# Two scalings by a column, the softmax division and the normalisation of the mLSTM heads, issued on ScalarE in a one-core hybrid attention block

## The chip, the cores and the metric

The kernel runs on one core of one Trainium2 chip. The metric is the device time of one execution in microseconds: the median over several runs. One execution was also taken with the hardware profiler. It has its own time and a span (first to last instruction), and the times of single instructions below come from it. PE is TensorE (matmuls), PEld its weight loads, DVE is VectorE, ACT is ScalarE, POOL is GpSimd, SP is SyncE, which only issues transfers here.

## What is computed

One layer of a decoder over 16 meta tokens and 512 tokens of width 1024. The normalised input goes through one wide projection. From its columns two branches are fed, and both end in one output projection. The parts that matter here:

```python
# branch 1: attention with forget gates, 8 heads of 128
p = jax.nn.softmax(jnp.where(causal, scores + decay, -jnp.inf), axis=-1)
out = jnp.einsum('bhqk,bkhd->bqhd', p, v)
ya = (oa * jax.nn.silu(fz)) @ w_a

# branch 2: mLSTM, 4 heads of 512 values
h = num / jnp.maximum(jnp.abs(den), jnp.exp(-m_t))[..., None]
hb = jax.nn.sigmoid(mo) * hb
hb = rms_norm(hb, g_head)                 # per head, over its 512 values
yb = (hb * jax.nn.silu(mz)) @ w_b

merged = jax.nn.sigmoid(ga) * ya + jax.nn.sigmoid(gb) * yb
return x + rms_norm(merged @ w_o, g_post)
```

The change concerns two steps: the division of the softmax by its row sums, and the multiplication of each mLSTM head with the reciprocal root of its mean square.

## The kernel before

Tokens stand on the 128 partitions in four chunks (c = 0 to 3), or channels do where a product is formed transposed. Every fp32 factor is split into a high part, rounded to the fp32 format that PE multiplies fast, and a low part. A product is three matmuls (`mm3`, L150 to L152): high by high, high by low, low by high. The high part is a copy on ACT (L142 or L250), the low part a subtraction on DVE (L144 or L252).

The program runs in this order: the norm of the input (to about 30 us), the four mLSTM heads h = 0 to 3 (to about 516 us), four pairs p = 0 to 3 of attention heads (FoX, to about 842 us), and the projections `w_a` and `w_o`. The instructions are written in the order of the functions, but a tile scheduler sorts them for each engine by what it expects to be ready. So an edit of one line can change the order on every engine. Each engine then works through its queue strictly in order, and waits with everything behind when an operand isn't there.

**mLSTM.** For one head, `value_part` is called with chunks (3, 2), then `mz_part(h, 0)` follows, then `value_part` with (1, 0), then `mz_part(h, 1)`. For each chunk `value_part` multiplies on PE (L790 to L793), divides by the denominator on DVE (L796 to L803, result `ht`), squares and sums on ACT (L807, result `mss`), scales the sum on DVE (L808), raises it to the power -0.5 on POOL (L810, result `mrs`), and multiplies `ht` by that column (L811). `turn_part` transposes the `ht` tiles on PE after the head's last chunk.

**Narrow projections.** `mz_part`, `fq_part`, `fz_part` and `gate_part` (names pz, pfq, pfz, pga, pgb) use `st_unit`, a Strassen form: seven products of half-size blocks instead of eight, with weight parts a, b, c, d. Between the products, ACT takes snapshots of half-finished banks (L314, L318, L322). PE may write on into a bank only when its snapshot is taken. At the end DVE combines the snapshots with the banks (L325, L326, L328).

**FoX.** For each head `prob_part` forms the logits (PE), adds the decay and finds the row minimum of their negation on DVE (L972, result `lt` and `mn`), takes the exponential with its row sum on ACT (L977, `rsum`), inverts the sum on DVE (L978), and writes the probabilities `pn`: the meta columns on POOL (L980), the others on DVE (L982, 128, 256, 384 or 512 columns for c = 0 to 3). `lt` has two buffers, so L972 of chunk c + 2 waits until L980 and L982 of chunk c have read theirs. `ptr_part` transposes `pn` on PE and copies it out on ACT (L1007, L1009; low parts on DVE, L1008, L1010). `fout_part` multiplies with the values (pfo, L1022 to L1024). A projection is placed beside each softmax to keep PE supplied: beside the last head (p = 3, m = 1) stands the gate `ga_part(1)`, behind it `ga_part(2)`. The sigmoids of a gate (L932) need another table on ACT than the exponential, hence an ACT_TABLE_LOAD.

Of the kernel before, what the change touches and what calls it, by code (L numbers as in the profile page):

```python
# [11 lines left out]
AF = mybir.ActivationFunctionType  # L12
ALU = mybir.AluOpType

P = 128
# [3 lines left out]
NM = 16  # L19
# [34 lines left out]
def tile_hybrid_block(ctx: ExitStack, tc: tile.TileContext, x, meta, norm_pre, norm_post, w_in, b_fox_f,  # L54
                      conv_w, conv_b, b_i, b_f, g_head, w_a, w_b, w_o, out):
    nc = tc.nc
    V, S, G, T = nc.vector, nc.scalar, nc.gpsimd, nc.tensor
# [11 lines left out]
    def psum1(name):  # L69
        return pa.tile([P, 512], F32, tag="pa", name=name)  # L70

    def banks(name, n):

        return [psum1(f"{name}_{i}") for i in range(n)]

    def line(pool, name, n=1, parts=P, **kw):

        return pool.tile([parts, -(-n // 16) * 16], F32, name=name, **kw)[:, 0:n]
# [19 lines left out]
    def sb(shape, dt, tag, name, pool=None, **kw):  # L98

        n = 1  # L100
        for d in shape[1:]:
            n *= d
        size = BYTES.get(tag, 4096)
        t = (pool or wk).tile([shape[0], size // (2 if dt == BF16 else 4)], dt, tag=tag, name=name, **kw)[:, 0:n]
        if len(shape) == 3:
            t = t.rearrange("p (a b) -> p a b", a=shape[1])
        elif len(shape) == 4:
            t = t.rearrange("p (a b c) -> p a b c", a=shape[1], b=shape[2])
        return t
# [39 lines left out]
    def mm3(ps, ah, al, bh, bl, start, stop, **kw):  # L149
        T.matmul(ps, ah, bh, start=start, stop=False, **kw)  # L150
        T.matmul(ps, ah, bl, start=False, stop=False, **kw)  # L151
        T.matmul(ps, al, bh, start=False, stop=stop, **kw)  # L152
# [628 lines left out]
    def value_part(h, wpk, v, so, hts, chunks):  # L781
        wh, wl = wpk
        vh, vl, vm = v
        for c in chunks:
            pn = (psum1(f"pna{h}{c}"), psum1(f"pnb{h}{c}"))
            for u in (1, 0):
                o, n = u * 256, 256 + 2 * u
                for j in range(c + 1):
                    s0 = OFF[j] + (c - j) * P
                    T.matmul(pn[u][:, 0:n], wh[:, s0:s0 + P], vh[:, j, o:o + n], start=(j == 0), stop=False)  # L790
                    T.matmul(pn[u][:, 0:256], wh[:, s0:s0 + P], vl[:, j, o:o + 256], start=False, stop=False)
                    T.matmul(pn[u][:, 0:n], wl[:, s0:s0 + P], vh[:, j, o:o + n], start=False, stop=False)
                T.matmul(pn[u][:, 0:n], wh[0:MP, OFFM + c * P:OFFM + (c + 1) * P], vm[0:MP, o:o + n],  # L793
                         start=False, stop=True)
            r = line(wk, f"r{h}{c}", 1, tag="r", bufs=4)
            V.tensor_scalar(r, pn[1][:, 256:257], -1.0, col[:, NB + NCH + c, 8 + h:9 + h], ALU.mult, ALU.max)  # L796
            V.tensor_tensor(r, pn[1][:, 256:257], r, ALU.max)
            V.reciprocal(r, r)
            if c % 2:
                ht2 = sb([P, 2, MV], F32, ("qk0h", "qk0l")[c // 2], f"ht{h}{c}")  # L800
            ht = ht2[:, c % 2, :]
            for u in range(2):
                V.scalar_tensor_tensor(ht[:, u * 256:u * 256 + 256], pn[u][:, 0:256], r,  # L803
                                       so[:, c, u * 256:u * 256 + 256], ALU.mult, ALU.mult)
            junk = sb([P, MV], BF16, "y", f"mjunk{h}{c}", bufs=2)
            ss = line(wk, f"mss{h}{c}", 1, tag="ss", bufs=8)
            S.activation(junk, ht, AF.Square, accum_out=ss)  # L807
            V.tensor_scalar(ss, ss, 1.0 / MV, EPS, ALU.mult, ALU.add)  # L808
            rs = line(wk, f"mrs{h}{c}", 1, tag="rs", bufs=7)
            G.tensor_tensor(rs, ss, mhalf, ALU.pow)  # L810
            V.tensor_scalar(ht, ht, rs, None, ALU.mult)  # L811
            hts[c] = ht

    def turn_part(h, hts, gz):
# [35 lines left out]
    for h in range(MH):  # L850
# [24 lines left out]
        else:  # L875
            wpk = score_part(h, q, k, w)
            so = mo_part(h)
        hts, gz = [None] * NCH, []
        value_part(h, wpk, v, so, hts, (3, 2))
        gz.append(mz_part(h, 0))  # L880
        value_part(h, wpk, v, so, hts, (1, 0))
        gz.append(mz_part(h, 1))
        pend = (h, hts, gz)
# [61 lines left out]
    def prob_part(p, m, q, k):  # L945

        h = 2 * p + m
        qh, ql = q
        kh, kl = k
        ab = sb([P, NA], F32, "ab", f"ab{h}", gp)  # L950
        nc.sync.dma_start(ab, d_na[h:h + 1, :].to_broadcast([P, NA]))
        pn = sb([P, NPACK], F32, "w", f"pn{h}")
        sums = []
        for c in range(NCH):
            kn = NM + (c + 1) * P
            o = OFFA[c] + kn - P
            G.tensor_tensor(ab[:, o:o + P], ab[:, o:o + P], mask_q, ALU.add)
            for s0, s1 in [(0, kn)] if kn <= 512 else [(0, HL), (HL, kn)]:

                if c != 1:  # L960
                    bank = psum1(f"pl{h}{c}{s0}")
                ps = (bank[:, 144:512] if c == 1 else bank)[:, 0:s1 - s0]
                mm3(ps, qh[:, m, c * P:(c + 1) * P], ql[:, m, c * P:(c + 1) * P],
                    kh[:, m, s0:s1], kl[:, m, s0:s1], True, True)
                sums.append((c, s0, s1, ps))
        for c in range(NCH):
            kn = NM + (c + 1) * P
            lt = sb([P, L], F32, "y", f"lt{h}{c}", bufs=2)
            mn = line(wk, f"mn{h}{c}", 2, tag="mn", bufs=4)
            parts = [(s0, s1, ps) for c_, s0, s1, ps in sums if c_ == c]  # L970
            for i, (s0, s1, ps) in enumerate(parts):
                V.tensor_tensor_reduce(out=lt[:, s0:s1], in0=ps, in1=ab[:, OFFA[c] + s0:OFFA[c] + s1],  # L972
                                       op0=ALU.add, op1=ALU.min, scale=1.0,
                                       scalar=3e38 if i == 0 else mn[:, 0:1], accum_out=mn[:, i:i + 1])
            li = len(parts) - 1
            rsum = line(wk, f"rsum{h}{c}", 1, tag="r", bufs=4)
            S.activation(lt[:, 0:kn], lt[:, 0:kn], AF.Exp, bias=mn[:, li:li + 1], scale=-1.0, accum_out=rsum)  # L977
            V.reciprocal(rsum, rsum)  # L978
            o = OFFP[c]
            G.tensor_scalar(pn[:, o:o + P].rearrange("p (g t) -> p g t", g=4),  # L980
                            lt[:, 0:32].unsqueeze(1).to_broadcast([P, 4, 32]), rsum, None, ALU.mult)
            V.tensor_scalar(pn[:, o + P:o + P + kn - NM], lt[:, NM:kn], rsum, None, ALU.mult)  # L982
        return pn

    def ptr_part(p, m, pn):
# [61 lines left out]
    for p in range(FH // 2):  # L1047
        if p:
            q = fq_part(p)
            if p % 2 == 0:  # L1050
                fout_part(*tail)
            k = fk_part(p)
        pn0 = prob_part(p, 0, q, k)
        if p % 2 == 0:
            v = fv_part(p)
        else:
            fz_part(p)
        pt0 = ptr_part(p, 0, pn0)
        pn1 = prob_part(p, 1, q, k)
        if p % 2 == 0:  # L1060
            fz_part(p)
        elif p == 1:
            gb_part(2)
        else:
            ga_part(1)
        fout_part(p, 0, pt0, v)
        pt1 = ptr_part(p, 1, pn1)
        tail = (p, 1, pt1, v)
        if p % 2 == 0:
            gb_part(p + 1)  # L1070
            fout_part(*tail)
# [57 lines left out]
    pn = banks("pout", NCH)  # L1129
# [7 lines left out]
    for u in (2, 3):  # L1137
        w = wchunk(wo, 0, KC, u * 256, 256, f"wo{u}")
        for b in range(NCH):
# [5 lines left out]
            if u == 3:  # L1145
                rs = line(wk, f"ors{b}", 1, tag="rs", bufs=7)
# [34 lines left out]
```

## Time and profile before

| what | value |
|---|---|
| median of 3 runs | 935.91 us (935.9 to 936.01) |
| profiled execution, its own time | 938.23 us |
| its span | 936.4 us |
| mean granted clock of PE | 0.995 |

In a group's row stands: line, engine, operation, output <- inputs, partitions x elements and type, count, then after the bar the busy us, the mean ns of one, the idle us of the engine just before, and what ended that. In a timeline's row stands: start in us, duration in us, engine, line, operation. A row of the waits names the waiting instruction, what released it, and the us in total, the number and the longest. Durations of neighbours on one engine overlap by some 0.1 us because they are pipelined. The mean clock of 0.995 comes from two stretches of 3.41 us at half clock, which begin at 104.41 and 691.50 us.

### The profile page before, as it was taken

To read this page: it belongs to the slowest core of one execution; us is meant where nothing else is said; L and a number is where in the kernel's file an instruction comes from. 1 tells how busy PE (TensorE), PEld (TensorE's weight loads), DVE (VectorE), ACT (ScalarE), POOL (GpSimd) and SP (SyncE) were. 2 spreads that over 40 slices of the span, in tenths; PEclk is the share of its full clock that TensorE was granted. 3 is DMA by queue.
4 is the path that set the end of the run, shared out by engine and by line. 5 is a ranking of instruction groups with operands and counts; after the bars stand their busy time and mean duration, and the time that the engine had idled before them with its cause. 6 is when DMAs were issued, how large, how long until landed. Compare 5 with 4: busy or idle time off the path is not lost.

```text
span 936.4 us, 15730 instructions
## 1 busy us (share of the span) xinstructions
PE 915.1 (98%) x6304; PEld 847.2 (90%) x6304; DVE 670.4 (72%) x1108; ACT 474.5 (51%) x810; POOL 141.6 (15%) x186
## 2 busy tenths in 40 slices
PE   8999899999999999999999999999989999999997
PEld 6998799889998899988999979899988999998887
DVE  6889688448886378873688767587894688995534
ACT  5645556536565255662455425455753464863231
POOL 3053000122101211012020002111421121300000
PEclk9999999999999999999999999999999999999999
DMA  7323133303333123233133335124352124358402
GB/s 230 93 63 118 46 127 90 111 23 91 109 95 101 51 85 91 95 97 90 33 104 112 96 109 162 49 77 152 101 166 76 56 87 136 98 193 302 135 23 91
DMA packets 73539, 97.47 MB, mean 104 GB/s; under 512 B 5237, under 2 KB 56533, under 8 KB 73466
## 3 DMA queue, kind: packets, MB, share of 16 engines
q1 hardware_dynamic: 71400, 92.76, 32.3%
q0 software_dynamic: 576, 2.10, 0.6%
q10 hardware_dynamic: 1490, 1.61, 0.5%
q8 instruction: 49, 0.80, 0.3%
q14 instruction: 24, 0.20, 0.1%
HBM read 90.62 MB, written 5.83 MB: 103 GB/s over the span
## 4 chain that ended last, share of the span: by engine, by line
PE 81%; DVE 9%; ACT 5%; issue 2%; DMA 2%; POOL 1%; DVEq 0%; POOLq 0%; ACTq 0%; SPq 0%
PE pyb L151 3%; PE pyb L150 3%; PE pyb L152 3%; PE pz L150 3%; PE pz L151 3%; PE pz L152 3%; PE pqk L150 3%; PE pqk L152 3%; PE pqk L151 3%; PE pv L150 3%; PE pv L152 3%; PE pv L151 3%; PE po L152 2%; PE po L150 2%; PE po L151 2%
## 5 line engine op out<-in xcount | busy, mean ns | idle before, releaser
L980 POOL TENSOR_SCALAR pn<-lt,rsum 128x128 f32<-128x128 f32 x32 | 29.5, 923 | 136.7 <-DVE rsum L978 99.6
L151 PE MATMUL pyb<-bl,wb_h 128*128 128x512 f32 x128 | 49.8, 389 | 0.0
L152 PE MATMUL pyb<-bh,wb_l 128*128 128x512 f32 x128 | 49.8, 389 | 0.0
L150 PE MATMUL pyb<-bh,wb_h 128*128 128x512 f32 x128 | 49.8, 389 | 0.0
L151 PE MATMUL pv<-wv_l,hh 128*128 128x512 f32 (+1 forms) x128 | 46.6, 364 | 1.5 <-DVE wv_l L144 1.5
L152 PE MATMUL pv<-wv_h,hl 128*128 128x512 f32 (+1 forms) x128 | 46.4, 363 | 0.0
L150 PE MATMUL pv<-wv_h,hh 128*128 128x512 f32 (+1 forms) x128 | 46.4, 362 | 0.0
L695 DVE SCALAR_TENSOR_TENSOR y<-z,gc,y 128x512 f32<-128x512 f32 (+1 forms) x48 | 36.2, 759 | 2.2 <-ACT y L688 1.4
L150 PE MATMUL pfk<-hh,wfk_h 128*128 128x264 f32 x128 | 36.4, 285 | 0.0
L150 PE MATMUL pqk<-hh,wq_h 128*128 128x258 f32 x128 | 36.4, 284 | 0.0
L150 PE MATMUL pqk<-hh,wk_h 128*128 128x264 f32 x128 | 36.3, 284 | 0.0
L151 PE MATMUL pfk<-hl,wfk_h 128*128 128x264 f32 x128 | 36.3, 283 | 0.0
L152 PE MATMUL pqk<-hh,wk_l 128*128 128x264 f32 x128 | 36.3, 283 | 0.0
L152 PE MATMUL pfk<-hh,wfk_l 128*128 128x264 f32 x128 | 36.3, 283 | 0.0
L151 PE MATMUL pqk<-hl,wk_h 128*128 128x264 f32 x128 | 36.2, 283 | 0.0
L152 PE MATMUL pqk<-hh,wq_l 128*128 128x258 f32 x128 | 36.0, 282 | 0.0
L151 PE MATMUL pqk<-hl,wq_h 128*128 128x258 f32 x128 | 36.0, 282 | 0.0
L151 PEld LDWEIGHTS pv<-wv_l,hh 128*128 128x128 f32 x128 | 24.1, 189 | 5.6 <-DVE wv_l L144 1.7
L152 PEld LDWEIGHTS pyb<-bh,wb_l 128*128 128x128 f32 x128 | 24.0, 188 | 5.0
L150 PEld LDWEIGHTS pyb<-bh,wb_h 128*128 128x128 f32 x128 | 24.0, 188 | 4.9
L151 PEld LDWEIGHTS pyb<-bl,wb_h 128*128 128x128 f32 x128 | 24.0, 188 | 4.9
L845 DVE TENSOR_TENSOR yb<-pyb,yb 128x512 f32<-128x512 f32 x24 | 16.5, 687 | 16.6 <-PE pyb L152 16.6
(1810 smaller groups left out, 3651.5 us busy)
## 6 DMA issues: line engine op xcount, KB each, us to landing
wv_r<-in_w_in_dram SPq DMA_DIRECT2D x16, 512.0 KB, 4.8
wo_r<-in_w_in_dram SPq DMA_DIRECT2D x16, 512.0 KB, 3.8
wz_r<-in_w_in_dram SPq DMA_DIRECT2D x16, 512.0 KB, 4.0
wb_r<-in_w_b_dram SPq DMA_DIRECT2D x16, 512.0 KB, 3.4
ab<-d_na SPq DMA_DIRECT2D x8, 672.0 KB, 4.0
wq_r<-in_w_in_dram SPq DMA_DIRECT2D x8, 512.0 KB, 3.9
wk_r<-in_w_in_dram SPq DMA_DIRECT2D x8, 512.0 KB, 4.7
wfq_r<-in_w_in_dram SPq DMA_DIRECT2D x8, 512.0 KB, 3.7
```

What stands on the lines that cost most here:

```text
L150: T.matmul(ps, ah, bh, start=start, stop=False, **kw)
L151: T.matmul(ps, ah, bl, start=False, stop=False, **kw)
L152: T.matmul(ps, al, bh, start=False, stop=stop, **kw)
L695: V.scalar_tensor_tensor(y[:, t0:L], z[:, m, t0 + j:L + j], gc[:, j * 16 + mi:j * 16 + mi + 1], y[:, t0:L], ALU.mult, ALU.add)
L845: V.tensor_tensor(dst, ps[i], dst, ALU.add)
L980: G.tensor_scalar(pn[:, o:o + P].rearrange("p (g t) -> p g t", g=4), lt[:, 0:32].unsqueeze(1).to_broadcast([P, 4, 32]), rsum, None, ALU.mult)
```

## The change

Two instructions of DVE become activations with the identity function on ACT; the scale is the same column as before. The operands, the tiles and the buffers stay.

```diff
@@ value_part
             G.tensor_tensor(rs, ss, mhalf, ALU.pow)
-            V.tensor_scalar(ht, ht, rs, None, ALU.mult)
+            S.activation(ht, ht, AF.Identity, scale=rs)
             hts[c] = ht
@@ prob_part
             G.tensor_scalar(pn[:, o:o + P].rearrange("p (g t) -> p g t", g=4),
                             lt[:, 0:32].unsqueeze(1).to_broadcast([P, 4, 32]), rsum, None, ALU.mult)
-            V.tensor_scalar(pn[:, o + P:o + P + kn - NM], lt[:, NM:kn], rsum, None, ALU.mult)
+            S.activation(pn[:, o + P:o + P + kn - NM], lt[:, NM:kn], AF.Identity, scale=rsum)
         return pn
```

This moves 16 instructions of L811 (4 heads, 4 chunks) and 32 of L982 (8 heads, 4 chunks). DVE has 48 rows fewer and ACT 48 more, 764 for 716. The count of table loads stays at 23. The scheduler also reorders what stands around them.

On ACT in mLSTM head 1, at the first half of `value_part` and the first snapshot of `mz_part` (ht13 and ht12 are the pair of chunks 3 and 2, gz10 the snapshot of the first `mz_part`), the order is now:

```order
 L758 ACTIVATE so1_2240<-po1_1_2242 128x2x256
 L807 ACTIVATE mjunk13_2506,mss13_2507<-ht13_2503 128x512
+L811 ACTIVATE ht13_2503<-ht13_2503,mrs13_2510 128x512
 L807 ACTIVATE mjunk12_2541,mss12_2542<-ht13_2503 128x512
+L811 ACTIVATE ht13_2503<-ht13_2503,mrs12_2545 128x512
 L314 ACTIVATE gz10_2548<-pz10_1_2550 128x512
 L250 ACTIVATE wz11c_h_2738<-wz111_r0_2728 128x1024
```

The two scalings stand ahead of the snapshot L314; before, it followed L807 directly.

On ACT behind the last softmax, between the gates ga1 and ga2 (sga1 is the sigmoid tile of ga1, wga2b_h and wga2c_h are high parts of the weights of ga2):

```order
 L1035 ACTIVATE gh1_9056<-yb_75 128x1024
 L322 ACTIVATE sga1_8767<-pga1_1_8769 128x256
-L250 ACTIVATE wga2b_h_8945<-wga20_r0_8935 128x1024
-L250 ACTIVATE wga2c_h_8949<-wga21_r0_8937 128x1024
 L932 ACT_TABLE_LOAD
 L932 ACTIVATE sga1_8767<-pga1_0_8768 128x512
@@ -664,21 +710,23 @@
 L1007 ACTIVATE pth7_8902<-pt73_8918 128x4x128
 L1009 ACTIVATE ptm7_8904<-pmt7_8905 128x512
+L250 ACTIVATE wga2b_h_8945<-wga20_r0_8935 128x1024
+L250 ACTIVATE wga2c_h_8949<-wga21_r0_8937 128x1024
```

Both splits move from a place ahead of the table load to one behind the sigmoids and the copies of the transposed probabilities.

On PE at ga1 (pfo6 is the attention output of head 6, pga1_1 the bank whose snapshot is taken on ACT):

```order
 L152 MATMUL pga1_0_8768<-hh_71,wga1c_l_8786 128x256
+L1022 MATMUL pfo6_8887<-pth6_8678,fvh2_7734 128x512
+L1023 MATMUL pfo6_8887<-ptl6_8679,fvh2_7734 128x512
+L1024 MATMUL pfo6_8887<-pth6_8678,fvl2_7735 128x512
+L1022 MATMUL pfo6_8887<-pth6_8678,fvh2_7734 128x384
+L1023 MATMUL pfo6_8887<-ptl6_8679,fvh2_7734 128x384
 L150 MATMUL pga1_1_8769<-t4h_1105,wga1c_h_8784 128x256
```

Five matmuls of the attention output come forward, ahead of the product that waits for the snapshot; at gb2 in pair 1 five of pfo2 do the same.

## The prediction

> **What bounds the kernel now.** I read the profile page first, then the waits of PE, then the groups by line and shape, and last the timelines of the places where the two moved operations stand.
>
> ```profile
> span 936.4 us, 15730 instructions
> ...
> PE 915.1 (98%) x6304; PEld 847.2 (90%) x6304; DVE 670.4 (72%) x1108; ACT 474.5 (51%) x810; POOL 141.6 (15%) x186
> ```
>
> PE is busy 98% of the span, so 936.4 - 915.1 = 21.3 us is all that it leaves open, start and end of the program included. DVE is at 72% and ACT at 51%: neither is the bound on average. The change can act only through the moments in which PE waits, and it can close or open such moments. The waits of PE, with total us, number and longest:
>
> ```profile
> PE pfq L150 <- ACT wfq2d_h L250: 1.9, 1, 1.9
> ...
> PE pfq L150 <- ACT fqs L314: 1.2, 3, 0.5
> ...
> PE pgb L150 <- DVE mn L972: 0.6, 1, 0.6
> PE pga L150 <- DVE mn L972: 0.5, 1, 0.5
> ```
>
> The waits are small and single. Several of them end with an ACT instruction: a weight split (L250) or a snapshot of a half-finished product (L314). PE cannot go on until ACT has taken the snapshot. So what counts on ACT is not its 51%, but what stands in its queue ahead of a snapshot or a split.
>
> **The price of the two operations.** Groups by line and shape; behind the bar are busy us, mean ns of one, and the idle time before:
>
> ```profile
> L811 DVE TENSOR_SCALAR ht<-ht,mrs 128x512 f32<-128x512 f32 x16 | 7.8, 487 | 8.7 <-POOL mrs L810 8.7
> ...
> L982 DVE TENSOR_SCALAR pn<-lt,rsum 128x512 f32<-128x512 f32 x8 | 4.0, 501 | 0.2
> ...
> L982 DVE TENSOR_SCALAR pn<-lt,rsum 128x128 f32<-128x128 f32 x8 | 2.3, 288 | 0.3
> ...
> L807 ACT ACTIVATE mjunk<-ht 128x512 bf16<-128x512 f32 x16 | 10.0, 625 | 12.5 <-DVE ht L803 12.5
> ...
> L687 ACT ACTIVATE z<-pqk 128x258 f32<-128x258 f32 x16 | 6.1, 381 | 12.8 <-PE pqk L152 12.7
> ...
> L688 ACT ACTIVATE y<-pqk,gc 128x258 f32<-128x258 f32 x16 | 8.7, 561 | 0.6 <-DVE bl L826 0.5
> ...
> L977 ACT ACTIVATE lt<-lt,mn 128x528 f32<-128x528 f32 x8 | 5.9, 734 | 8.4 <-DVE mn L972 8.4
> ...
> L977 ACT ACTIVATE lt<-lt,mn 128x144 f32<-128x144 f32 x8 | 3.3, 417 | 3.5 <-DVE mn L972 3.5
> ```
>
> DVE loses 16 instructions of 0.487 us at L811, 7.8 us. At L982 it loses 8 each of four widths, from 0.288 us (128 wide) to 0.501 us (512 wide): by the mean of the ends, 32 x 0.39 = 13 us. On ACT the same passes are longer. No activation of before has exactly the new form (512 wide, SBUF to SBUF, scale from a column), so I bound it. L807 is 512 wide with no column operand: 0.625 us. L688 has two column operands (scale and bias) and L687, of the same shape, none: (561 - 381) / 2 = 90 ns for one. So L811 should take 0.625 + 0.09 = 0.71 us, between 0.63 (the column costs nothing) and 0.81 (it costs as much as both). L977 already takes one column operand, and its 528 and 144 columns are 16 more than L982 has. The step per column is (734 - 417) / 384 = 0.83 ns, so L982 takes 0.72 us at 512 and 0.40 at 128, and by the same step 0.50 and 0.62 between. ACT gains 16 x 0.71 + 8 x 2.24 = 29 us, far within its idle half. None of this is on the path by itself.
>
> **First term: L811 ahead of the snapshot L314 in heads 1, 2 and 3.** In the first half of value_part (chunks 3 and 2), ACT squares a chunk (L807), DVE and POOL make the reciprocal root, and the scaling follows. After that comes the snapshot. Timeline of head 1, ACT, POOL, DVE and PE (start us, us):
>
> ```profile
> 238.29 0.63 ACT L807 ACTIVATE mjunk<-ht 128x512 bf16<-128x512 f32 x1 [0.76 <-DVE ht L803]
> ...
> 238.92 0.58 ACT L314 ACTIVATE gz<-pz 128x512 f32<-128x512 f32 x1
> ...
> 239.28 0.55 POOL L810 TENSOR_TENSOR mrs<-mss,mhalf 128x1 f32<-128x1 f32 x1 [0.78 <-DVE mss L808]
> ...
> 238.53 0.49 DVE L811 TENSOR_SCALAR ht<-ht,mrs 128x512 f32<-128x512 f32 x1 [0.28 <-POOL mrs L810]
> ...
> 241.22 0.29 PE L150 MATMUL pz<-t4h,wz10c_h 128*128 128x256 f32 x1
> ```
>
> Before, ACT goes from L807 straight to L314, which ends at 239.50. PE starts the product that overwrites the snapshot's bank at 241.22, so there are 1.72 us to spare. In the new order L811 stands behind each L807 and ahead of L314. ACT can start L811 of chunk 3 when DVE could, at 238.53, and ends it at 239.24. L807 of chunk 2 then starts at 239.15 (pipelined by some 0.1 us, as 238.29 + 0.63 and 238.92 leave no gap with the accumulator read between), 0.86 later than before. POOL's root came 239.28 - 238.29 = 0.99 after it and took 0.55, so it is ready at 240.69. ACT waits for it with L314 queued behind; L811 of chunk 2 runs to 241.40, and L314 ends about 241.91. PE is ready at 241.22: a stall of 0.7 us, 0.5 with L811 at 0.63 and 0.9 at 0.81. Head 2 has the same order. Head 3 has one weight split more, which fits into the wait for POOL. In head 0 it is different:
>
> ```profile
> 114.37 0.60 ACT L314 ACTIVATE gz<-pz 128x512 f32<-128x512 f32 x1 [1.12 <-PE pz L152]
> ```
>
> There L314 waits for PE itself and ACT is idle 1.12 us before it, so both scalings fall into idle time. The second half (chunks 1 and 0) delays the snapshot L318 by one L811 at most, and the last L811 stands behind L318; I take 0, with 0.7 a head as the upper bound. Sum: 3 x 0.7 = **+2.1 us**, between 1.5 and 4.
>
> **Second term: the softmax chains of FoX get shorter on DVE.** POOL's small copy at L980 reads the same buffer (ns minimum/median/maximum), and the ACT timeline of the first of the places:
>
> ```profile
> L980 POOL TENSOR_SCALAR pn<-lt,rsum x32: 600/898/1817, 579.6 to 814.5; 128x128 f32<-128x128 f32 x32
> ```
>
> ```profile
> 610.30 0.74 ACT L977 ACTIVATE lt<-lt,mn 128x528 f32<-128x528 f32 x1 [2.30 <-DVE mn L972]
> ...
> 611.99 0.36 ACT L318 ACTIVATE yb<-pfz 128x256 f32<-128x256 f32 x1
> ```
>
> ACT sits idle 2.30 us for L972, the DVE pass that forms the logits. L972 needs one of two lt buffers, so it follows the last reader of the buffer, and DVE has its own L982 and the reciprocals in between. With L982 gone from DVE, L972 of chunks 2 and 3 comes earlier. In exchange one ACT pass of 0.62 and one of 0.72 us stand ahead of L318, partly in the 2.30 idle. My balance is a snapshot some 0.4 us earlier in pairs 0 and 2, which takes about 0.35 off the wait of pfq for fqs that ends each of these stretches (0.5 at most, quoted above): **-0.7 us**, between 0 and -1.2. In pairs 1 and 3 the snapshot behind the chain comes some 1.2 us later, but the new order puts five matmuls of the attention output ahead of the product that waits: 0.
>
> **Third term: the split wga2b_h at the end of pair 3.** The last softmax (head 7) lies beside the two gate projections ga1 and ga2. Timeline of ACT, DVE and PE:
>
> ```profile
> 814.38 0.36 ACT L322 ACTIVATE sga<-pga 128x256 f32<-128x256 f32 x1
> ...
> 816.36 1.06 ACT L250 ACTIVATE wga2b_h<-wga_r 128x1024 fp32r<-128x1024 f32 x1 [1.62 <-DVE wga_r L261]
> ...
> 818.39 1.28 ACT L932 ACT_TABLE_LOAD   x1
> 819.68 1.09 ACT L932 ACTIVATE sga<-pga 128x512 f32<-128x512 f32 x2
> ...
> 821.19 0.98 ACT L1007 ACTIVATE pth<-pt 128x384 fp32r<-128x384 f32 x2
> 822.06 0.60 ACT L1009 ACTIVATE ptm<-pmt 128x512 fp32r<-128x512 f32 x1
> ```
>
> ```profile
> 816.85 0.69 DVE L328 TENSOR_TENSOR pga<-pga,sga 128x512 f32<-128x512 f32 x1
> ```
>
> ```profile
> 820.14 0.28 PE L150 MATMUL pga<-t3h,wga2b_h 128*128 128x256 f32 x1
> ```
>
> Before, wga2b_h is split at 816.36, and PE uses it at 820.14: 2.7 us of cover. The new order lets ACT do the table load, both sigmoids, the three L1007 and L1009 first. By how much? The four passes of head 7 add 2.24 us to ACT, of which about 0.6 falls into idle time, so L322 ends 1.65 later, at 816.4. DVE, which no longer has L982 in the way, finishes L328 at about 817.85 (817.54 before). The table load and the two sigmoids take 2.38 from there (818.39 to 820.77), to 820.2, and the four copies another 2.0 (820.65 to 822.66), to 822.2. Then the split ends at about 823.2. PE stands ready at about 820.25, so it waits 2.95 us. If the table load does not wait for L328, everything is 1.3 us earlier and the stall is 1.65. Six matmuls of the last attention output come forward into the product behind, but they stand behind the first use of wga2b_h and do not fill this gap. I take **+2.9 us**, from 1.6 to 3.2.
>
> **The sum.** 2.1 - 0.7 + 2.9 = +4.3 us. The span goes from 936.4 to 940.7, the profiled execution from 938.23 to 942.5, and since it lies 2.3 over the median of 935.91, the median goes to **940.2**.
>
> **Rivals.** The first is one more clock dip. Stretches of the trace (us, busy us with counts of PE, PEld, DVE, ACT, POOL, then the granted clock):
>
> ```profile
> 538.00:539.70 1.70, 0.43 (x4) 0.23 (x3) 0.39 (x1) 1.05 (x3) 0.00 (x0) 1.00 0.83 258
> 688.00:692.10 4.10, 1.49 (x11) 1.08 (x10) 2.92 (x5) 2.45 (x3) 0.00 (x0) 0.93 0.62 224
> 691.50:694.90 3.40, 2.88 (x13) 2.88 (x14) 3.40 (x4) 2.66 (x5) 0.00 (x0) 0.50 0.53 142
> 694.90:698.30 3.40, 3.40 (x26) 3.23 (x25) 3.30 (x5) 2.07 (x4) 0.00 (x0) 1.00 0.96 339
> ```
>
> A gap of 1.27 us near 538 left the clock at 1.00. Where PE worked only 1.49 of 4.1 us, the next 3.4 us were granted 0.50, and 13 matmuls ran in the time of 26: a loss of 1.7 us. A gap of 2.9 us lies nearer to the second. With a dip the median is 940.2 + 1.7 = 941.9. A rule speaks against it: the Trainium skill, "TensorE: Matmul & The Clock Gate", section "What's actually happening", puts the half rate after at least one idle window of about 3.4 us, so a gap of 2.9 us would leave 940.2. This trace has already dipped after less idleness than a full window, so I keep the rival. Chance 0.25, against 0.43 for the forecast without it.
>
> The second: only the heads' stalls come, because ACT or PE reach the place of wga2b_h otherwise than I walked it and the split is hidden again. Then +2.1 - 0.7 = +1.4, 937.3. For it speaks that 2.7 us of cover were there before; against it, the order. Chance 0.12.
>
> The third: the change is off the path altogether. L811 takes 0.63, the snapshots come in time, and FoX stays as it is: 935.9, give or take 1. For it speaks ACT at 51%. Chance 0.11.
>
> The fourth ends on the other side: the relief of DVE and POOL wins in FoX. While DVE runs L982, POOL's L980 takes up to 1817 ns where it can do 600. If all L980 fall to 600, lt is freed up to 0.3 us earlier by the median, 1.2 by the longest, and L972 with it. Then the waits quoted above go: 1.2 + 0.6 + 0.5 = 2.3 us, and 933.6 if the stalls of the first and third term are hidden; if the 1.9 of wfq2d_h and the dip behind it (1.7) go too, 930.0. It decides from the point where heads and split together cost less than 2.3 us. Against it: I find three new stalls by name. Chance 0.09. The Trainium skill, "SBUF — State Buffer", section "SBUF: two separate sides", describes a shared port pair of VectorE and GpSimd that one of them holds for a whole instruction; by that rule this rival's 933.6 would follow wherever L982 and L980 now overlap, and the spread of L980 from 600 to 1817 agrees with it.
>
> **How the numbers follow.** Two runs of this kernel can be told apart from about 0.2%, 1.9 us, so "same" is 934.0 to 937.8. Forecast and dip (0.68) are slower; of the second rival two thirds are same (0.08) and one slower (0.04); the third is same (0.11); the fourth is faster (0.09). That is faster 0.09, same 0.19, slower 0.72. For the range, the terms at their low ends give 1.5 - 1.2 + 1.6 = +1.9; the third rival's centre takes it down to 935.8. At the top, the forecast's terms at 2.7 - 0.4 + 3.2 are +5.5, and the dip at the forecast +6.0: 942.0, and half of the terms' spread more, 943.0.
>
> **What would show it.** Right: PE waits on ACT gz L314 of about 0.7 in heads 1, 2 and 3 and none in head 0; L811 at 0.71 us on ACT and L982 from 0.40 to 0.72; one wait of pga for wga2b_h near 3 us; the fqs waits smaller. Wrong: no wait at gz, a wga2b_h split done before 820, L980 near 600 with the mn waits gone, or a second stretch at clock 0.50 behind the new gap.

## The result: slower by 0.7%, and the profile after

The changed kernel takes **941.93 us** (median; 940.28 to 943.43), the kernel before 935.9 beside it. The ratio is 1.0069, with a 95% interval of 1.0051 to 1.0086. By that ratio it is 6.5 us more (4.8 to 8.0); the two medians are 6.0 apart. I had forecast 940.2, from 935.8 to 943.0. The sign and the range held. The sum behind them held less well, as the runs below show. The profiled execution of the changed kernel took 940.28 us, the least of its four runs.

The page of the kernel after, its span and its engines:

```profile
span 938.5 us, 15743 instructions
...
PE 916.1 (98%) x6304; PEld 847.4 (90%) x6304; DVE 653.4 (70%) x1060; ACT 497.8 (53%) x858; POOL 135.6 (14%) x186
```

DVE lost 17 us, ACT gained 23 and POOL lost 6. PE is as busy as before, and none of the others is near a bound on average. So the loss must stand in the waits of PE and in its clock. After the change they are:

```profile
PE pnb L790 <- ACT wh L729: 2.7, 2, 2.0
PE pga L150 <- ACT wga2b_h L250: 2.1, 1, 2.1
PE pz L150 <- ACT gz L314: 1.8, 3, 0.6
PE pfq L150 <- ACT wfq2d_h L250: 1.7, 1, 1.7
...
PE pga L150 <- ACT sga L314: 0.8, 2, 0.4
...
PE pga L150 <- ACT sga L318: 0.4, 1, 0.4
...
PE pfq L150 <- ACT fqs L314: 0.2, 1, 0.2
```

Two large waits are new: gz L314, three times 0.6 us, and wga2b_h, 2.1 us. Those are the two stalls of the forecast, by name, count and place. Two are smaller: fqs from 1.2 to 0.2 (forecast) and sga L318 from 1.3 to 0.4 (not forecast). The two waits for mn, 0.6 and 0.5 before, are gone (the fourth rival). The wait for wfq2d_h is nearly as in the profile of before, 1.7 for 1.9, and that is the trap in this case: the third batch of runs shows why.

The prices, in the groups by line and shape (busy us, mean ns of one):

```profile
L811 ACT ACTIVATE ht<-ht,mrs 128x512 f32<-128x512 f32 x16 | 11.6, 725 | 10.3 <-POOL mrs L810 10.3
...
L982 ACT ACTIVATE pn<-lt,rsum 128x512 f32<-128x512 f32 x8 | 5.7, 708 | 0.0
...
L982 ACT ACTIVATE pn<-lt,rsum 128x128 f32<-128x128 f32 x8 | 3.1, 389 | 0.8 <-DVE rsum L978 0.8
```

Forecast were 0.71 for L811, 0.72 and 0.40 for the two ends of L982; measured are 0.725, 0.708 and 0.389.

The first stall in head 1, timeline of ACT, then of PE:

```profile
238.30 0.73 ACT L811 ACTIVATE ht<-ht,mrs 128x512 f32<-128x512 f32 x1 [1.00 <-POOL mrs L810]
238.93 0.61 ACT L807 ACTIVATE mjunk<-ht 128x512 bf16<-128x512 f32 x1
...
240.49 0.72 ACT L811 ACTIVATE ht<-ht,mrs 128x512 f32<-128x512 f32 x1 [0.85 <-POOL mrs L810]
241.12 0.58 ACT L314 ACTIVATE gz<-pz 128x512 f32<-128x512 f32 x1
```

```profile
240.87 0.28 PE L152 MATMUL pz<-hh,wz10c_l 128*128 128x256 f32 x1
241.75 0.38 PE L150 MATMUL pz<-t4h,wz10c_h 128*128 128x256 f32 x1 [0.59 <-ACT gz L314]
```

ACT stands idle 0.85 us for POOL's root with L314 queued behind. L314 could have run in that gap. It ends at 241.70, and PE goes on at 241.75.

### The profile page after: what moved, and what is told of

Same layout as the page of the kernel before. It is cut to its first block, busy times and chain, and to the rows that moved or that the text cites. A ratio compares the mean times of both kernels' runs of the same rounds, so it can differ in the third digit from the quotient of the medians.

```text
span 938.5 us, 15743 instructions
## 1 busy us (share of the span) xinstructions
PE 916.1 (98%) x6304; PEld 847.4 (90%) x6304; DVE 653.4 (70%) x1060; ACT 497.8 (53%) x858; POOL 135.6 (14%) x186
## 4 chain that ended last, share of the span: by engine, by line
PE 78%; DVE 9%; ACT 7%; DMA 2%; issue 2%; POOL 1%; SPq 0%; DVEq 0%; POOLq 0%; ACTq 0%
PE pyb L152 3%; PE pyb L150 3%; PE pyb L151 3%; PE pqk L150 3%; PE pqk L152 3%; PE pqk L151 3%; PE pv L152 3%; PE pv L150 3%; PE pv L151 3%; PE pz L150 2%; PE pz L152 2%; PE pz L151 2%; PE po L152 2%; PE po L150 2%; PE po L151 2%
## 5 line engine op out<-in xcount | busy, mean ns | idle before, releaser
L980 POOL TENSOR_SCALAR pn<-lt,rsum 128x128 f32<-128x128 f32 x32 | 19.1, 603 | 131.5 <-DVE rsum L978 92.9
L144 DVE TENSOR_TENSOR wo_l<-wo_r,wo_h 128x1024 fp32r<-128x1024 f32 x12 | 15.9, 1335 | 16.9 <-ACT wo_h L142 16.9
```

The costliest lines, as they stand in the source:

```text
L144: pin(V.tensor_tensor(lo, raw, f(hi), ALU.subtract))
```

## First batch: which part costs what

The theory then: what costs is what stands ahead of a snapshot or a split. The rival: ScalarE simply has too much to do, and the loss goes with the time added to it. Four kernels take the parts apart. Their times stand beside 935.16 for the kernel before (24 runs). In this and the later batches the edits are shown shortened: `...` stands for what is left out, and some helper lines are written out more plainly.

**Normalisation alone.** The division goes back to VectorE.

```diff
-            S.activation(pn[:, o + P:...], lt[:, NM:kn], AF.Identity, scale=rsum)
+            V.tensor_scalar(pn[:, o + P:...], lt[:, NM:kn], rsum, None, ALU.mult)
```

> Only the normalisation (L811) stands on ScalarE; the softmax division is back on VectorE. Stall theory: three waits of PE on gz L314 of about 0.6 us in heads 1, 2 and 3, +2.4 us up to the end of head 3, of which the wait of pga on sga L318 (1.3 us before) gives back about 1.0 to 1.2; no wait on wga2b_h. Net +1.2: median about 937.1 beside 935.9 (936.5 to 938.5 with the clock). Rival 1 (heads hidden, the whole loss is the last softmax): no gz waits, 935.9. Rival 2 (the loss is spread over ScalarE, wherever it has more to do): about 0.38 of 6.0, as 11.6 of the 30 us that ScalarE gained are L811: 938.2.

Measured: 937.01, ratio 1.0019 (1.0010 to 1.0028). The three gz waits are there, 1.8 us in sum. The loss of 1.8 us is between the 1.2 of the theory and the 2.3 of rival 2, so the time alone doesn't tell them apart; the waits do. Rival 1 falls.

**Division alone.** The normalisation goes back.

```diff
-            S.activation(ht, ht, AF.Identity, scale=rs)
+            V.tensor_scalar(ht, ht, rs, None, ALU.mult)
```

> Only the softmax division (L982) stands on ScalarE; the normalisation is back on VectorE. Stall theory: no gz waits; L980 at 0.60 us, fqs waits near 0.2 us, -2.0 us through pairs 0 to 3; then one wait of pga on wga2b_h of about 2 us, +0.7 at the gate behind it, and a stretch at half clock after it (+1.7): net +1.0 without and +2.4 with the half clock, so 937 to 939. Rival 1 (the whole loss is the last softmax): 941 to 942. Rival 2 (loss by ScalarE's added time): 935.9 + 0.62 x 6 = 939.6.

Measured: 940.85, ratio 1.0060 (1.0048 to 1.0072): two to four us more than the theory gave, and nearest to rival 1, which gave the whole loss to the last softmax. Something in the softmax part was missing from the account.

**All but the last softmax.**

```diff
-            S.activation(pn[...], lt[:, NM:kn], AF.Identity, scale=rsum)
+            S.activation(pn[...], ..., scale=rsum) if h < 7 else V.tensor_scalar(pn[...], ...)
```

> The whole change, but the softmax division of head 7 alone (4 of 32 instructions) is back on VectorE. Stall theory: no wait on wga2b_h and no half clock near 820; three gz waits of 0.6 stay. +1.2 for the heads, -2.0 for pairs 0 to 3: 935.1 (934 to 936.5 with the clock). Rival 2 (loss by ScalarE's added time): 2.2 of 30 us less on ScalarE, so 941.5.

Measured: 938.27, ratio 1.0030 (1.0019 to 1.0041). Four instructions of 48, 2.2 us of ACT, are worth 3.7 us. So the loss is not spread over ACT's time. But 938.27 is 3 us over the theory's 935.1: again something is missing.

**Without both stalls.** In addition, the normalisation of chunks 3 and 2 in heads 1 to 3 is back.

```diff
+            S.activation(ht, ...) if h == 0 or c < 2 else V.tensor_scalar(ht, ...)
+            S.activation(pn[...], ...) if h < 7 else V.tensor_scalar(pn[...], ...)
```

> The change without its stalls: the division of head 7 and the normalisation of chunks 3 and 2 of heads 1, 2 and 3 (10 instructions of 48) are back on VectorE. Stall theory: neither gz waits nor a wait on wga2b_h; only the gain of pairs 0 to 3 is left: 935.9 - 2.0 = 933.9 (932.5 to 935 with the clock), faster than both kernels. Rival 2 (loss by ScalarE's added time): 6.6 of 30 us less, 940.6. Rival 3 (the gain of the pairs is only a lucky clock of one profile): 935.9.

Measured: 934.06, ratio 0.9994 (0.9982 to 1.0006). Ten instructions back on VectorE, and the loss is gone. Six of them, those of the heads, are worth 938.27 - 934.06 = 4.2 us. Rival 2 (940.6) falls. But its single runs spread widely, from 932.31 to 937.81, and its profile is the slowest of them. The third batch names a loss that only some of its runs may have, so the 4.2 can hold more than the heads.

## Second batch: the same work in another order

If order is what counts, all 48 passes can stay on ScalarE and the stalls still go. The kernel before had 935.35 here (12 runs).

**Normalisation behind the snapshot.**

```diff
-            S.activation(ht, ht, AF.Identity, scale=rs)
+            late.append((ht, rs))
...
-        gz.append(mz_part(h, 0))
+        gz.append(mz_part(h, 0)); scale_late(snapped[-1].ins)   # L811 queued behind L314
```

> The whole change, all 48 passes on ScalarE, but each pair of normalisations (L811) is queued behind the snapshot L314 of its projection, not ahead of it. ScalarE has the same work to the instruction. Stall theory (what counts is what stands ahead of a snapshot): the three gz waits go, and the time falls from 941.9 by 2.4 to 4.2: 938.5 (937.5 to 939.5); the wait on wga2b_h stays near 2. Rival (ScalarE has too much to do in the heads, wherever it stands): 941.9 and waits of another name instead.

Measured: 938.8, ratio 1.0041 (1.0028 to 1.0053). The same call follows `mz_part(h, 1)`. ACT in head 1 (L811 is L813 in this kernel's file):

```profile
238.81 0.58 ACT L314 ACTIVATE gz<-pz 128x512 f32<-128x512 f32 x1
239.29 1.32 ACT L813 ACTIVATE ht<-ht,mrs 128x512 f32<-128x512 f32 x2
```

The gz waits are gone, with ACT's work the same to the instruction: 3.1 us. For the heads the order is the cause.

**Split ahead of the sigmoids.** The weights of ga2 are loaded and split before the sigmoids of ga1 are issued, and the latter are queued behind the split wga2b_h.

```diff
+        if (name, u) == ("ga", 1): ahead["ga2"] = st_narrow(C_GA + 512, "wga2", V)
+        with tc.issue_after(cut_hi["wga2b"].ins):      # for ga1 only
             for m in range(2): S.activation(sg[:, m, :], ps[m], AF.Sigmoid)
```

> The whole change, but the weight splits of ga2 are made ahead of the sigmoids of ga1, so that wga2b_h stands ahead of the table load again, as before the change. All passes stay on ScalarE. Stall theory: no wait on wga2b_h, no half clock near 820, the three gz waits stay; as taking the last softmax off ScalarE: 938.3 (937 to 939.5). Rival (the four passes of the last softmax cost time on ScalarE wherever the split stands): 941 to 942, with a wait of pga on another split or snapshot of about 2 us.

Measured: 940.81, ratio 1.0060 (1.0048 to 1.0072). The theory's 938.3 is a miss; the time lies next to the rival's 941 to 942. The waits of this kernel show what happened:

```profile
PE pga L150 <- ACT sga L314: 1.5, 2, 1.2
...
PE pga L152 <- DVE wga2b_l L252: 1.0, 1, 1.0
...
PE pga L152 <- DVE wga3b_l L252: 0.6, 1, 0.6
```

The wait for wga2b_h went, and in its place came one for the low part of the same split, one for a snapshot (1.2) and one for the next gate's split, together 2.8 us behind the last softmax. The same place cost 2.5 in after: 2.1 for wga2b_h and 0.4 for sga L314. So at this place the order alone isn't the cause: with the four passes of head 7 on ACT the other order passed the wait on. Whether a third order would do better isn't shown.

**Both orders at once.**

> Both reorderings at once: normalisations behind the snapshots, splits of ga2 ahead of the sigmoids, all 48 passes on ScalarE. Stall theory: near the version without the two stalls that had 10 passes back on VectorE (934.06): 934.5 (933 to 936), level with the kernel before (935.2) or a little faster. Rival (the passes themselves are too long for ScalarE): 940 to 942.

Measured: 938.37, ratio 1.0030 (1.0019 to 1.0041): the gain of the first order (2.4 us against the kernel just above, 3.1 where it stood alone), little from the second. The forecast of 934.5 rested on the second and missed with it.

**The gap filled.** 18 matmuls are issued ahead of the product that waits; their results are overwritten. (The matmuls of head 7's output are held behind that product.)

```diff
         prod("X", "a11", "b11")
+        for _ in range(18):                            # ga2 only
+            T.matmul(units[0][0][:, 256:512], w_hi, t_hi, start=True, stop=True)
```

> The whole change in its own order, with 18 matmuls of 256 columns added on TensorE right ahead of the product that waits for wga2b_h, about 2.1 us; they write into a bank that the next product overwrites. They add work and fill the gap. If the half clock near 820 follows from TensorE's idleness: no stretch at 0.50 near 820, the split still ends when it did, and the time falls by up to 1.7: 940.5 (939.5 to 941.5). Rival (the half clock has another cause, or costs nothing): a stretch near 820 again or no gain, 941.9 to 943.

Measured: 940.68, ratio 1.0056 (1.0044 to 1.0068). Here are the stretches near 820 of after, then of this kernel (us; busy us of PE, PEld, DVE, ACT, POOL; granted clock):

```profile
817.00:820.90 3.90, 1.76 (x15) 1.55 (x14) 3.78 (x7) 3.90 (x8) 0.00 (x0) 1.00 0.33 134
820.96:824.30 3.34, 3.34 (x15) 3.05 (x14) 3.34 (x4) 1.97 (x3) 0.00 (x0) 0.50 0.00 0
824.40:827.80 3.40, 3.40 (x31) 3.40 (x31) 2.93 (x5) 0.89 (x3) 0.00 (x0) 1.00 0.49 155
```

```profile
817.00:820.90 3.90, 3.90 (x35) 3.87 (x34) 3.84 (x7) 3.77 (x7) 0.00 (x0) 1.00 0.14 58
820.96:824.30 3.34, 2.62 (x20) 2.21 (x20) 3.28 (x5) 3.34 (x5) 0.00 (x0) 1.00 0.20 82
```

In after, PE is busy 1.76 of 3.90 us, and the next 3.41 us come at half clock: 15 matmuls, where 31 run in the 3.40 us behind it. With the gap filled the clock stays at 1.00. One profile is no proof, as the kernel with the normalisation behind the snapshot has the same wait of 2.1 us and kept 1.00 too (the last section shows why). Over all fourteen profiles the link is clear: of the four with this wait three have a stretch at half clock behind it (after, the division alone, and a kernel of the third batch), of the ten others none. By the start times of the same matmuls PE gains 1.3 us here against after. The medians differ by 1.25 us (941.93 - 940.68), which lies inside their intervals. So 1.3 us is my estimate of what the half clock costs here, less the time of the added matmuls; the rest is the wait.

## Third batch: the loss that I had not listed

The account was still some 2 to 4 us short for the division alone and for all but the last softmax, and the gain that I expected in the pairs seemed to be missing. The wait for wfq2d_h points to the place. It is at the end of pair 1, where DVE's L266 builds a weight sum for wfq2d and POOL's L939 multiplies gate gb2. Timeline of POOL and DVE in after:

```profile
678.20 2.39 POOL L957 TENSOR_TENSOR ab<-ab,mask_q 128x128 f32<-128x128 f32 x4 [1.92 <-DMA ab<-d_na]
683.96 2.39 POOL L939 TENSOR_TENSOR yb<-yb,sgb 128x1024 f32<-128x1024 f32 x1 [3.37 <-ACT sgb L932]
```

```profile
683.99 2.92 DVE L266 TENSOR_TENSOR wfq_r<-wfq_r,wfq_r 128x512 f32<-128x512 f32 x1
```

L266 starts 0.03 us behind L939 and takes 2.92 us instead of 0.69: it ends 0.56 us after L939 does. The Trainium skill, "SBUF — State Buffer", section "SBUF: two separate sides", says that a GpSimd operation and certain VectorE operations (among them those with two SBUF inputs, where the GpSimd one reads SBUF) exclude each other for the whole instruction. Both operations here read two tiles of SBUF, and the trace agrees with the rule in its size: L266 ends when L939 has ended and most of its own 0.69 us has passed. The normalisation alone shows the other side: there L266 starts 0.13 us ahead and takes 0.68 us, and L939 takes 2.82 instead of 2.40. The four runs of this batch stand beside 935.2 for the kernel before (27 runs).

**The kernel before, once more.**

> The kernel before, unchanged, for a second profile and more times. Clash theory: in most of its runs VectorE's pass L266 on wfq2 starts ahead of GpSimd's pass L939 and takes 0.69 us, and the first profile of before, at 938.23 above all 36 timed runs, was one in which L939 came first and L266 took 2.92. So the new profile should show L266 at 0.69, a wait of pfq on wfq2d_h of 0.5 or none and no half clock near 691; 935.2. Rival (the first profile is the usual run and profiling adds 2 us): L266 at 2.92 again, the waits of 1.9 and 0.8 again, and a profiled time near 938.

Measured: 935.04, ratio 1.0004 (0.9995 to 1.0013). The new profile of the same kernel, POOL and DVE:

```profile
681.35 3.15 POOL L957 TENSOR_TENSOR ab<-ab,mask_q 128x128 f32<-128x128 f32 x4 [2.85 <-DMA ab<-d_na]
684.46 2.40 POOL L939 TENSOR_TENSOR yb<-yb,sgb 128x1024 f32<-128x1024 f32 x1
```

```profile
683.41 0.77 DVE L266 TENSOR_TENSOR wfq_r<-wfq_r,wfq_r 128x512 f32<-128x512 f32 x1
```

Now POOL is held by the masks of the next pair (L957) until 684.5. L939 comes behind L266, and L266 takes 0.77 us. The wait for wfq2d_h and the half clock near 691 are gone; the execution took 934.59, inside the timed runs. The first profile of before had this:

```profile
680.68 2.69 POOL L957 TENSOR_TENSOR ab<-ab,mask_q 128x128 f32<-128x128 f32 x4 [2.31 <-DMA ab<-d_na]
683.55 2.40 POOL L939 TENSOR_TENSOR yb<-yb,sgb 128x1024 f32<-128x1024 f32 x1 [0.17 <-ACT sgb L932]
```

```profile
683.58 2.92 DVE L266 TENSOR_TENSOR wfq_r<-wfq_r,wfq_r 128x512 f32<-128x512 f32 x1
```

There the masks ended at 683.37 and L939 got in first, by 0.03 us: at 938.23 that was an untypical run, as the timed runs of this kernel, in all batches, lie between 933.9 and 936.98. I had taken its 2.3 us over the median for an offset of the profile. It was the clash. With the division on ScalarE the softmax chain ends sooner, the masks run at 678.2, POOL is free in time, and L939 comes first: the change's own gain opens the clash. In all eight profiles so far with the division on ScalarE (wholly, or without head 7), the longest L266 on wfq took 2.90 to 2.92 us; with the normalisation alone on ScalarE it took 0.68. (Of the kernel without both stalls the profiled run, 937.81, was the slowest of twelve, so there the clash needn't be the rule.)

**The change, with L939 held behind L266.**

```diff
-        G.tensor_tensor(y, y, sg, ALU.mult)            # gb2: traced behind fq_part(2)
+        m = G.tensor_tensor(y, y, sg, ALU.mult)
+        tc.add_manual_dep(m.ins, adds["wfq2"].ins.name, Sync)
```

> The whole change; in addition GpSimd's pass L939 of gate gb2 waits for VectorE's L266 on wfq2, so that it can't come first. The work is the same. Clash theory (with the division on ScalarE, L266 reaches its place just after L939, in every profile so far; that is a part of the loss that I had not listed): L266 at 0.69, the waits on wfq2d go from 2.5 to about 0.5, the half clock near 692 goes in most runs: 941.9 - 2.2 to - 3.9, so 939 (937.5 to 940). Rival (the place has slack, or another wait stands behind): 941 to 942.

Measured: 937.84, ratio 1.0026 (1.0017 to 1.0035). One wait of an off-path operation, and 4.1 us come back. POOL and DVE at this place (L939 is L940 here):

```profile
684.39 2.39 POOL L940 TENSOR_TENSOR yb<-yb,sgb 128x1024 f32<-128x1024 f32 x1 [3.68 <-DVE wfq_r L266]
```

```profile
683.56 0.69 DVE L266 TENSOR_TENSOR wfq_r<-wfq_r,wfq_r 128x512 f32<-128x512 f32 x1
```

The waits for wfq2d are 0.4. This profile has no half clock near 691, and that of after has none there either; between these two PE gains 2.3 us at this place. One stretch of half clock (1.7) would make it 4.0, close to the 4.1 of the medians. Of the nine profiles with the long L266, eight have such a stretch near 691, of the five without it none. After's own profile is the one that was spared, and its other three runs had mean clocks of 0.992 to 0.995 against 0.996; which stretches they had, no trace shows.

**All remedies.** Normalisation behind the snapshots, head 7's division on VectorE, L939 behind L266; 44 of 48 passes on ScalarE.

> 44 of the 48 passes on ScalarE: the normalisations behind the snapshots, the division of heads 0 to 6; the division of head 7 on VectorE; and L939 of gb2 behind L266. If stalls, half clock and clash are all of the loss, what is left is the gain of the softmax chains: 934.1 (the version without the two stalls) less 2 to 3: 931.5 (930 to 933), faster than both kernels. Rival (the clash has slack): 934.

Measured: **930.47**, ratio 0.9954 (0.9942 to 0.9967), faster than both kernels, by 4.3 us against before (3.1 to 5.4). Its longest waits:

```profile
PE pnb L790 <- ACT wh L729: 2.3, 2, 1.7
PE pv L151 <- DVE wv_l L144: 1.5, 1, 1.5
PE warm L120 <- DVE wsrc L113: 1.4, 1, 1.4
PE pnb L792 <- DVE wl L731: 0.7, 1, 0.7
PE pga L150 <- ACT sga L314: 0.6, 1, 0.6
```

The waits for gz, wga2b_h, wfq2d_h and fqs are gone.

**The control.** The same dependency in the kernel before:

> The kernel before with the one addition that L939 of gb2 waits for L266 on wfq2. Clash theory: most runs of before have no clash, so 935.2 (934.5 to 935.5), no gain. Rival (before has the clash in most runs): 932 to 933, and then the gain of the version with all remedies is not the change's.

Measured: 935.65, ratio 1.0005 (0.9996 to 1.0013). The dependency alone brings before nothing. The gain of the version with all remedies is the change's.

The three losses, each taken alone out of the changed kernel: 941.93 - 938.80 = 3.1 (heads), 941.93 - 938.27 = 3.7 (last softmax), 941.93 - 937.84 = 4.1 (clash), together 10.9. Take that from 941.93 and 931.0 is left; with all three out, 930.47 was measured. The parts add up better than one may ask of medians whose single runs spread by 2 to 4 us: all three differences hang on the same four runs of the changed kernel, whose interval is 1.6 us to either side, and the others were taken in later batches. So the change gains 4 to 5 us and loses about 11, with 1 to 2 us of doubt in each.

## Why the prediction came out, step by step

- **Prices.** Right to 0.02 us, by the rows of L807, L687, L688 and L977.
- **First term, heads (+2.1).** The mechanism is shown by the reordered kernel. Waits of 0.6 where I had 0.7, three, none in head 0. By the start times of the same matmuls PE lost 0.84 to 0.96 in each head, restart included, 2.8 in all. Taken out, the term was worth 3.1 (2.4 in the pair of reordered kernels): up to one third too small.
- **Second term, chains (-0.7).** The mechanism is right and the size far off. POOL's L980 fell as the fourth rival said, here in after (ns minimum/median/maximum):

```profile
L980 POOL TENSOR_SCALAR pn<-lt,rsum x32: 592/603/629, 580.6 to 810.3; 128x128 f32<-128x128 f32 x32
```

  From 898 to 603, and the fqs waits to 0.2. By the two profiles with equal half-clock stretches (the kernel with all remedies against the control), PE comes earlier by 2.4 us over the four pairs. Another 1.35 comes ahead of the pairs: 0.4 at 512, and 0.95 at 539, where the wait for sga L318 shrinks whenever the normalisation is off VectorE (1.2 in the control, 0.3 with all remedies). I had not walked these places, and their chains aren't followed here either. In all the gain is 3.7 us by these profiles and 4.3 (3.1 to 5.4) by the timed runs, the fourth rival's order of size, not mine. That rival came true beside the stalls and not in their place, as I had put it; the second and third rivals fell.
- **The place near 690, which the sum left out.** The prediction didn't list it as a cost; it took the waits of wfq2d_h and the half clock for a part of the kernel before and gave them only to the fourth rival. They were a part of one execution. And it added the 2.3 us between that execution and the median back as if they were fixed. This step failed, by 4.1 us, and cancelled most of what the second term had too little.
- **Third term, last softmax (+2.9).** The wait came as walked: the split ended behind the sigmoids and copies. That the order alone makes it was wrong, as the kernel with the split ahead shows.

```profile
815.31 1.28 ACT L932 ACT_TABLE_LOAD   x1 [1.44 <-DVE pga L328]
...
819.45 1.07 ACT L250 ACTIVATE wga2b_h<-wga_r 128x1024 fp32r<-128x1024 f32 x1
```

  The table load did wait for L328, as I took it. From there to the end of the split it took 5.2 us (forecast 5.35). The wait was 2.1, not 2.95, as ACT and DVE reached L328 earlier against PE. With the half clock the term was worth 3.7.
- **Rival of the half clock (0.25).** It came true in the profile, at 820.96. The rule of the Trainium skill ("TensorE: Matmul & The Clock Gate", section "What's actually happening": half rate after at least one idle window of about 3.4 us) didn't hold here: the longest gap of PE was 2.14 us, and it had been busy 1.76 of the 3.90 us ahead. The row of before that spoke against the rule (1.49 busy of 4.1, then 0.50) was the better guide.
- **The total.** Forecast +4.3, measured +6.5 (4.8 to 8.0). The terms were +2.1, -0.7 and +2.9; the runs give +3.1, +3.7, +4.1 and a gain of 4 to 5. The stalls were foreseen, but that the sum came near was luck: a gain that was too small stood against a loss that was missing. The profiles show it. The span was to go from 936.4 to 940.7 and went to 938.5, because the profile of before already had the clash and a half clock behind it. Against the second profile of before, by the start times of the same matmuls, the heads cost 2.8, the clash 2.4 and the place behind the last softmax 4.4, half clock included; 1.3 comes back ahead of the pairs and 2.2 in them.

## What to carry to other kernels

On an engine with half its time free, ask of a moved operation what is queued behind it: here a snapshot behind a scaling that waits for POOL cost more (2.8 us) than the relief of VectorE brought (1.3 us, behind the heads), and the same scaling behind the snapshot cost no wait there. Before a profile is taken as the kernel, hold its own time against the timed runs: here 938.23 against a median of 935.91 came from one wait that was rare, and the forecast carried its price along as if it were fixed. A gain that lets one engine run ahead can set it against another, as L266 and L939 here, so look for two passes of VectorE and GpSimd that start within a few hundredths of a microsecond.

## What the runs showed of the hardware

- Half clock comes in steps. Apart from the one at the end of every execution, behind the last matmul, its stretches last 3.413 us or twice that, and within one execution their starts lie whole multiples of 3.413 apart (before: 104.41 and 691.50, 172 steps; after: 104.16 and 820.96, 210 steps). The phase differs from run to run, so the same gap gives one stretch, two or none: at 104 us the profiles show one (before) or two (before again, 6.83 us). That is probably a part of the spread of the timed runs. The stretch at the end (before: from 933.85) also counts in before's mean clock of 0.995, beside the two named at the start.
- What counts is how busy PE is in one window of this grid. Laid on it, the fourteen profiles have 3639 windows at full clock between 20 and 915 us. All 21 in which PE was busy less than 48% were followed by half clock, none that was busy more than 58%, and 4 of the 17 between. Two windows of after (near 818 and near 688), then two in a row of the kernel with the normalisation behind the snapshot:

```profile
817.55:820.96 3.41, 1.27 (x11) 1.06 (x10) 3.29 (x6) 3.41 (x7) 0.00 (x0) 1.00 0.37 154
...
687.84:691.25 3.41, 1.71 (x16) 1.52 (x14) 2.23 (x5) 1.20 (x2) 0.00 (x0) 1.00 0.91 308
```

```profile
815.48:818.89 3.41, 1.67 (x15) 1.47 (x13) 3.32 (x6) 3.41 (x7) 0.00 (x0) 1.00 0.37 154
818.89:822.31 3.42, 3.10 (x22) 2.82 (x23) 3.39 (x4) 2.90 (x5) 0.00 (x0) 1.00 0.00 0
```

  Behind the first, busy 1.27 us, came half clock; behind the second, busy 1.71, it didn't. In the other kernel the wait of 2.1 us fell across the edge of two windows, and the clock stayed at 1.00.
- Two passes that start 0.03 us apart decide 2.2 us: L266 at 0.69 to 0.77 us ahead of L939, 2.92 behind it.
- GpSimd's L980 loses a third of its time (898 to 603 ns in the median) when VectorE no longer runs a pass over the same tile beside it.
